# The stores of the input projection and of the gates issued from ScalarE's queue instead of the sync engine's

## The chip, the cores and the metric

One core of a Trainium2 chip runs the whole kernel. The metric is device time in microseconds (us) of one execution, from its first to its last work; below it is called the time. The core has engines that each take their own instructions in order: TensorE (PE, with PEld for its weight loads), VectorE (DVE), ScalarE (ACT), GpSimd (POOL) and the sync engine (SP), which computes nothing and only issues transfers. A transfer (DMA) is an instruction in one engine's queue; the data is moved afterwards by 16 DMA engines. An instruction that waits holds up everything behind it on its own engine.

## The reference

One layer of a decoder trunk, for 2048 tokens of width 1024, all in float32. Cut to what matters:

```python
mod = cond @ w_ada[l] + b_ada[l]
shift1, scale1, gate1, shift2, scale2, gate2 = jnp.split(mod, 6, axis=-1)
h = modulated_rmsnorm(x, norm_mix[l], shift1, scale1)
z = h @ w_in[l]
(gq, gk, gv, glow, gout, hq, hf, hi, hout,
 mqk, mv, mi, mf, mout) = jnp.split(z, IN_OFFSETS, axis=-1)
mixed = jnp.concatenate([gla_group(...), hgrn2_group(...), mlstm_group(...)], axis=-1)
x = x + gate1[:, None] * (mixed @ w_out[l])
h = modulated_rmsnorm(x, norm_mlp[l], shift2, scale2)
ff = jnp.square(jax.nn.relu(h @ w_ff1[l])) @ w_ff2[l]
x = x + gate2[:, None] * ff
return _rms(x) * final_norm
```

The three groups are recurrent token mixers (gated linear attention twice, mLSTM once), computed chunk by chunk. `z` is the input projection; its columns are activated (sigmoid, silu, a short convolution) before the mixers use them.

## The kernel before

The 2048 tokens are worked on in four quarters of 512. First comes the input projection of all four quarters (`inproj`), then the output projection and the feed-forward network of each quarter (`outproj`, `f1`, `f2`). The token mixing of a quarter (`block_pass`, `gates`, `chunk`) is emitted in small steps beside these dense products (`pump`), and a scheduler sets the final order on every engine from its own estimates of when each instruction could start; `ahead()` gives the dense products' casts and evacuations a preference over the mixing.

A dense product is done in three passes over operands split into a high and a low part. `weights` loads a piece into a buffer `raw` (two of them, L184, SP), ScalarE casts it to its high part in `wt` (three buffers, L176), and VectorE takes the rest (L177), which frees `raw`. The input projection has nine groups of columns for each quarter (f, q, conv, hout, gout, m, gqk, hi, gv). For one group, four PSUM banks `ps_ip` (four buffers of `psd`) collect the four tiles of 128 tokens over four pieces of weights; the next group's first products need the first bank back. `evac` empties a bank: ScalarE's activations and, for some groups, VectorE's products write a buffer `st` (three buffers for all groups), and a DMA `dma_s` stores it to DRAM (`zq`, `zv`, `zg`; `zm` from the convolution, and `gn` from `gla_gate`), where the token mixing later reads it. An `st` buffer is free for the next tile only when its store has landed. The stores are:

- group f: L765 and L766, behind VectorE's L763 and L764
- group q: L771, behind VectorE's L736 (`silu`) and L769; `gla_gate`: L869, behind ScalarE's L868
- conv: L751, behind VectorE's L750
- gout: L791, behind VectorE's L736; hout: L791, behind ScalarE's L787
- m: L779 and L780, gqk: L775, hi and gv: L784, all behind ScalarE's own copies and activations

Over the four quarters these are 184 transfers. The token mixing's loads and stores go through GpSimd's queue (`dma_m`), the loads of weights, of x and of the modulation weights through the sync engine's (`dma`). The norm of the next quarter is made beside the projection: L701 loads x (`m<-xq`) and ScalarE squares it in L208 and L210.

Of the kernel before, what the change touches and what calls it, by code (L numbers as in the profile page):

```python
# [101 lines left out]
def trunk(ctx, tc, I, out):  # L102
# [3 lines left out]
    dma_m = G.dma_start  # L106
    dma_s = nc.sync.dma_start

# [41 lines left out]
    def ahead():  # L150
        """What the dense products wait for goes before the token mixing in each engine's order."""
        return tc.high_priority(offset=lead[0])
# [4 lines left out]
    def late():  # L157
        """Products of the token mixing give way to so many instructions that came after them."""
        return tc.high_priority(offset=-LATE)

# [8 lines left out]
    def ln_exp(after):  # L169
        """The set with Exp and Ln, behind the activation after; what the caller adds to the stack runs behind it."""  # L170
        with tc.issue_after(after.ins):
            p_ = A.preload_act_table_set("natural_log_exp_and_others")
        return tc.issue_after(p_.ins)
# [5 lines left out]
    def weights(src, n, lp=None):  # L179
        """A [128, n] piece of weights as its two parts, [128, 2, n]."""  # L180
        with ahead():
            raw = wp.tile([P, 1024], F32, tag="raw", name="raw", bufs=2)
            r = raw[:, 0:n]
            dma(out=r, in_=src)  # L184
            wt = (lp or wp).tile([P, 2, 1024], F32R, tag="wt", name="wt", bufs=4 if lp else 3)
            split(wt[:, 0, 0:n], wt[:, 1, 0:n], r)
        return wt[:, :, 0:n]
# [10 lines left out]
    def modulate(hi, lo, src, rs, a_, b_, tmp=None):  # L198
        """hi + lo = src * a_ * rs + b_; the product goes to src's place if there is no tmp."""
        tmp = src if tmp is None else tmp  # L200
        V.scalar_tensor_tensor(out=tmp, in0=src, scalar=a_, in1=rs, op0=ALU.mult, op1=ALU.mult)
        A.activation(out=hi, in_=tmp, func=AF.Identity, bias=b_)  # L202
        V.scalar_tensor_tensor(out=lo, in0=tmp, scalar=b_, in1=hi.bitcast(F32), op0=ALU.add, op1=ALU.subtract)

    def sq_acc(sm, src, first, over=False):
        """Adds src ** 2 (to be kept in src's place if over) and its share of EPS to sm."""
        if first:
            return A.activation(out=sm, in_=src, func=AF.Square)  # L208
        sq = src if over else m5()[:, 0:src.shape[-1]]
        last = A.activation(out=sq, in_=src, func=AF.Square)  # L210
        V.scalar_tensor_tensor(out=sm, in0=sm, scalar=EPS / 7 * KT, in1=sq, op0=ALU.add, op1=ALU.add)
        return last

    def newton(x, y, t, scale):
        """One step of y towards (x * scale + EPS) ** -0.5; x and t are overwritten."""
        V.tensor_scalar(out=x, in0=x, scalar1=scale, scalar2=EPS, op0=ALU.mult, op1=ALU.add)
# [14 lines left out]

    # ---------------------------------------------------------------- conditioning
    ada_tags, acc_tags = [], ["prod", "sdt", "alb"]

    def ada(m, o, n, slow=False):
        """Channels o .. o + n of modulation vector m; slow: in steps and beside the rest, in the buffers of those."""
        h, o_ = divmod(o, 512)
# [37 lines left out]

    # ---------------------------------------------------------------- token mixing
    R.sd = [dp.tile([TQ, 576], F32, name=f"sd{q}") for q in range(NQ)]
# [15 lines left out]
    def block_pass(q, s):  # L293
        """Scores of tokens at most 15 apart within blocks of 16 tokens, for 48 channels per group."""
        c0 = (lambda g: 96 * g + 48 * s) if s < 2 else (lambda g: 384 + 48 * g)
# [26 lines left out]
    def gates(q):  # L322
        """mLSTM gate rows of a quarter (row 32 n + h: chunk n, head h): running stabiliser and what follows."""
        g = gm[q]
# [76 lines left out]
    def chunk(q, n, L, N):  # L401
        """Up to the normalised outputs of chunk n; N is the next chunk of the quarter."""
        nxt = (lambda f: f(q, n + 1, N)) if N else (lambda f: None)
        pt = lambda nm: psm.tile([P, 512], F32, tag="psm", name=nm)
        # channel-major q, k, f
        X = m1.tile([P, 15, 128], F32, tag="X", name="X")
# [64 lines left out]
        yield  # L471
        # mLSTM scores
        gT = [R.gT[:, i, n, :] for i in range(4)]
# [22 lines left out]
        yield  # L496
        # diagonal blocks of the gated groups' scores
        dsum = m1.tile([P, 12, 16], F32, tag="dsum", name="dsum")
# [7 lines left out]
        nxt(load_sd)  # L506
        # mLSTM output
        psi = pt("ps_mi")
# [35 lines left out]
        yield  # L544
        # scores of the gated groups
        heads = [(h // 2, 64 * (h % 2), 64) for h in range(6)] + \
# [69 lines left out]
        V.tensor_reduce(out=ss[:, 0:6], in_=sq, op=ALU.add, axis=AX.X)  # L616
        # norms, output gates
        with ln_exp(last):
# [35 lines left out]
    def both(a, b):  # L654
        """The steps of two independent generators by turns."""
        its = [a, b]
# [19 lines left out]

    # ---------------------------------------------------------------- input projection
    PASSES = ((0, 0), (0, 1), (1, 0))
# [33 lines left out]
    def h_stats_slow(q, res):  # L712
        """The same for quarter q in steps, its loads a step ahead."""
        sm = stat("sm", 2)
# [15 lines left out]
    def inproj(q, hts, nxt):  # L730
# [62 lines left out]
        def part(g, c0, n, ps, kk):  # L793
            """Two k-tiles' share of n columns of a group (of n // 128 channel tiles of the convolution)."""
            kind = GROUPS[g][0]
# [74 lines left out]

    # ---------------------------------------------------------------- output projection and feed-forward
    R.x1 = [dp.tile([P, KT, TQ], F32, name=f"x1{q}") for q in range(NQ)]

    def spare(spec, src):
        """Eight [128, 512] tiles in buffers that the chunks leave free, loaded from src."""
        ts = []
# [56 lines left out]
    def ffn_in(h2, q, xs, sm, last, lp=None):  # L933
        """The feed-forward's input into the list h2, in steps."""
        rs = stat("rs", 1)
# [35 lines left out]
    def f2_tile(hds, b, acc, w, dt, c):  # L971
        """Block b's share of channel tile dt for the tokens c of a quarter; w: from the number of a part to the part."""
        n, nf = c.stop - c.start, NF[b]
# [32 lines left out]
    def final_steps(q, acc):  # L1006
        """The final norm of a quarter, in steps."""
        sm = stat("sm", 2)
# [10 lines left out]
    def f2_last(lp, hds, acc):  # L1019
        """The last block and the final norm by halves of the tokens, the first norm beside the second half's products."""  # L1020
        ws = [w2_part(LB, i, lp) for i in range(NF[LB])]
# [14 lines left out]

    # ---------------------------------------------------------------- schedule
    prog = _K()
# [25 lines left out]
    def step():  # L1064
        """One step of the block passes (which run ahead) or of the chunks."""
        can_b = prog.blocks < prog.ready and prog.us >= prog.loaded
# [9 lines left out]
    def pump(us):  # L1076
        """Token mixing beside us of dense products, at the pace that the nearest deadlines ask for."""
        prog.us += us
# [110 lines left out]

# How the emission of the token mixing is paced beside the dense products, in us of the tensor engine's dense work  # L1190
# where the comment gives no other unit.
SLACK = (20, 60, 60, 60)    # by which a quarter's mixing is to be done before it is due
LAST = 1480                 # when the last quarter's mixing is due
FILL = 20.0                 # mixing emitted behind the first quarter's output projection
LOAD = 5.0                  # from a block pass's loads to its arithmetic
RUN = 0.2                   # share of the next quarter's block passes that goes beside a quarter's chunks
AHEAD = 60                  # instructions by which weights and evacuations go before the mixing
LATE = 20                   # instructions by which the mixing's products give way
STATS = 14                  # step of the input projection at which the next quarter's norm starts
BG = (24, 12, 20)           # steps of the input projection beside which the other modulation vectors are made  # L1200
EARLY = 3                   # feed-forward block of the last but one quarter behind which the last one's x1 is made
_OUT_SHAPE = (4, P, KT, TQ)
# [18 lines left out]
```

## Time and profile before

| what | value |
|---|---|
| time, median of 3 runs | 2723.67 us (2722.57 to 2724.44) |
| profiled execution: span | 2721.9 us |
| TensorE busy in the span | 2636.9 us (97%) |
| VectorE busy | 1792.1 us (66%) |
| ScalarE busy | 1231.6 us (45%) |
| GpSimd busy | 259.2 us (10%) |
| DMA | 401.76 MB, mean 148 GB/s |

The profiled execution is one run of its own; its own time is its span, 2721.9 us, which is 1.8 us below the median of the three timed runs. Times in the profile's rows count from the start of this span. A row of waits reads "who <- whom: us in total, times, longest"; a row of the timeline gives start, duration, engine, line, operation, tiles written and read, and in square brackets how long the engine sat idle before it and what released it. SPq is the sync engine's queue of transfers. The input projection fills the first 850 us or so; the rest is output projection and feed-forward.

### The profile page before, as it was taken

The page shows a single profiled execution, that of the slowest core. Times are in us where ns is not written, and L with a number is a line of the kernel's source. Part 1 is how long each engine was busy: PE and PEld are TensorE (multiplying, and loading weights), DVE is VectorE, ACT ScalarE, POOL GpSimd, SP SyncE. Part 2 cuts the span into 40 slices and gives each one's busy share as a digit, 9 for nine tenths or more (in the row PEclk, how much of TensorE's full clock was granted, in tenths as well). Part 3 has the DMA queues.
Part 4 walks back from the last instruction along what each step waited for, and adds up shares of the span by engine and source line. Part 5 has one row for each costly group of instructions (what it writes and reads, how often), then busy time and mean ns, then how long its engine had stood idle before and what let it go on. Part 6 is the DMA issues. An engine that isn't in the chain of part 4 may idle for free.

```text
span 2721.9 us, 39555 instructions
## 1 busy us (share of the span) xinstructions
PE 2636.9 (97%) x15050; PEld 2212.7 (81%) x15050; DVE 1792.1 (66%) x3345; ACT 1231.6 (45%) x2190; POOL 259.2 (10%) x434
## 2 busy tenths in 40 slices
PE   6999999999999999999999999999999999999998
PEld 5888898898888777788877888788877788888887
DVE  8785687977776877776887655457556556533335
ACT  4654445445543543454453445345445543433333
POOL 0101110020201102112110000100000000000000
PEclk9999999999999999999999999999999999999999
DMA  8776675585547424445454333344433245342332
GB/s 259 222 227 185 176 238 167 174 231 176 160 140 217 116 82 135 126 133 165 132 177 125 118 120 113 117 140 146 145 119 111 89 129 176 107 146 93 95 99 78
DMA packets 160200, 401.76 MB, mean 148 GB/s; under 512 B 20473, under 2 KB 60490, under 8 KB 160010
## 3 DMA queue, kind: packets, MB, share of 16 engines
q1 hardware_dynamic: 129338, 306.51, 35.7%
q0 software_dynamic: 30672, 92.73, 12.4%
q8 instruction: 118, 1.93, 0.3%
q14 instruction: 72, 0.59, 0.1%
HBM read 336.21 MB, written 62.95 MB: 147 GB/s over the span
## 4 chain that ended last, share of the span: by engine, by line
PE 50%; DVE 2%; ACT 1%; DMA 1%; issue 0%; DVEq 0%; ACTq 0%; SPq 0%
PE ps_f L155 40%; PE ps_op L155 5%; PE ps_a L163 2%; DVE wt L177 1%; DMA raw<-w 1%; PE ps_oh L163 1%; PE ps_og L163 1%; PE ps_t L167 0%; PE ps_x L167 0%; DVE acc L1000 0%; PE ps_mv L163 0%; ACT wt L176 0%; PE ps_uh L163 0%; PE ps_ug L163 0%; PE ps_ms L155 0%
## 5 line engine op out<-in xcount | busy, mean ns | idle before, releaser
L155 PE MATMUL ps_f<-ht,wt 128*128 128x512 f32 (+1 forms) x5472 | 1307.9, 393 | 4.8 <-ACT ht L202 4.8
L155 PEld LDWEIGHTS ps_f<-ht,wt 128*128 128x128 f32 x5472 | 1003.9, 189 | 213.4 <-ACT ht L202 5.0
L177 DVE TENSOR_TENSOR wt<-raw,wt 128x1024 fp32r<-128x1024 f32 (+3 forms) x436 | 498.8, 1145 | 412.8 <-ACT wt L176 411.7
L176 ACT CAST wt<-raw 128x1024 fp32r<-128x1024 f32 (+3 forms) x436 | 431.4, 990 | 640.1 <-PE ps_f L155 345.3
L155 PE MATMUL ps_ip<-wt,ht 128*128 128x384 f32 (+2 forms) x3072 | 604.5, 353 | 32.9 <-ACT st L782 8.7
L155 PEld LDWEIGHTS ps_ip<-wt,ht 128*128 128x128 f32 x3072 | 550.4, 191 | 61.1 <-ACT st L782 10.3
L982 DVE SCALAR_TENSOR_TENSOR acc<-ps_f,mod,acc 128x512 f32<-128x512 f32 (+1 forms) x200 | 145.2, 727 | 129.2 <-PE ps_f L155 128.4
L962 ACT ACTIVATE m<-ps_f 128x512 f32<-128x512 f32 x128 | 76.7, 599 | 318.5 <-PE ps_f L155 318.2
L155 PE MATMUL ps_f<-h,wt 128*128 128x512 f32 x768 | 181.4, 397 | 0.0
L155 PEld LDWEIGHTS ps_f<-h,wt 128*128 128x128 f32 x768 | 144.6, 188 | 35.6 <-issue 0.5
L155 PE MATMUL ps_op<-ht,wt 128*128 128x512 f32 x576 | 133.1, 393 | 5.7 <-ACT ht L176 3.8
L155 PEld LDWEIGHTS ps_op<-ht,wt 128*128 128x128 f32 x576 | 108.8, 190 | 29.2 <-ACT ht L176 3.9
L301 POOL DMA_DIRECT2D blk<-zq x144 | 93.6, 663 | 344.1 <-DVE prod L311 204.2
L567 DVE TENSOR_TENSOR td<-ps_a,td 128x384 f32<-128x384 f32 (+2 forms) x96 | 40.6, 423 | 110.8 <-PE ps_a L163 110.3
L311 DVE TENSOR_TENSOR prod<-blk 128x768 f32<-128x768 f32 (+3 forms) x192 | 111.2, 579 | 2.9
L312 DVE TENSOR_REDUCE Sd<-prod 128x48 f32<-128x768 f32 (+3 forms) x192 | 110.5, 575 | 3.0
L965 DVE TENSOR_TENSOR ht<-m,ht 128x512 fp32r<-128x512 f32 x128 | 88.1, 688 | 22.8 <-ACT m L964 22.3
L310 DVE TENSOR_TENSOR blk<-blk 128x720 f32<-128x720 f32 (+4 forms) x180 | 98.9, 549 | 0.0
L155 PE MATMUL ps_ip<-ht,wt 128*128 128x512 f32 x384 | 98.4, 404 | 0.0
L155 PEld LDWEIGHTS ps_ip<-ht,wt 128*128 128x128 f32 x384 | 71.4, 191 | 14.9 <-issue 0.7
L964 ACT ACTIVATE m<-m 128x512 f32<-128x512 f32 x128 | 81.0, 633 | 2.6
L963 ACT ACTIVATE ht<-m 128x512 fp32r<-128x512 f32 x128 | 81.1, 634 | 0.1
(393 smaller groups left out, 2627.2 us busy)
## 6 DMA issues: line engine op xcount, KB each, us to landing
raw<-w SPq DMA_DIRECT2D x256, 512.0 KB, 3.5
raw<-wg SPq DMA_DIRECT2D x100, 384.0 KB, 3.8
m<-wada SPq DMA_DIRECT2D x64, 256.0 KB, 3.7
raw<-wo SPq DMA_DIRECT2D x32, 512.0 KB, 3.5
m<-xq SPq DMA_DIRECT2D x56, 256.0 KB, 3.3
raw<-wg SPq DMA_DIRECT2D x28, 512.0 KB, 4.4
blk<-zq POOLq DMA_DIRECT2D x144, 96.0 KB, 6.1
zt<-zq POOLq DMA_DIRECT2D x48, 288.0 KB, 3.9
```

Source lines behind the costliest of these rows:

```text
L155: T.matmul(out=ps, lhsT=l, rhs=r, start=start, stop=stop)
L163: T.matmul(out=ps, lhsT=l, rhs=r, start=start, stop=stop)
L176: A.copy(out=hi, in_=src)
L177: V.tensor_tensor(out=lo, in0=src, in1=hi.bitcast(F32), op=ALU.subtract)
L301: dma_m(out=t[i][32 * g:32 * g + 32], in_=src)
L310: V.tensor_tensor(out=t[1][:, 0:n, :], in0=t[1][:, 0:n, :], in1=t[2][:, d:16, :], op=ALU.mult)
L311: V.tensor_tensor(out=prod[:, 0:n, :], in0=t[1][:, 0:n, :], in1=t[0][:, d:16, :], op=ALU.mult)
L312: V.tensor_reduce(out=s49[:, 0:n, d:d + 33:16], in_=prod[:, 0:n, :].rearrange("p j (u c) -> p j u c", c=16), op=ALU.add, axis=AX.X)
L963: A.activation(out=hd[:, 0], in_=r, func=AF.Square)
L964: A.activation(out=r, in_=r, func=AF.Square)
L965: V.tensor_tensor(out=hd[:, 1], in0=r, in1=hd[:, 0].bitcast(F32), op=ALU.subtract)
L982: V.scalar_tensor_tensor(out=acc[:, dt, c], in0=ps, scalar=mod[:, 40 + dt:41 + dt], in1=acc[:, dt, c], op0=ALU.mult, op1=ALU.add)
```

## The change

One name is bound to another queue: `dma_s`, which issues the stores listed above, becomes ScalarE's `dma_start`.

```diff
     V, A, G, T = nc.vector, nc.scalar, nc.gpsimd, nc.tensor
     dma = nc.sync.dma_start
     dma_m = G.dma_start
-    dma_s = nc.sync.dma_start
+    dma_s = A.dma_start
```

No arithmetic, no buffer and no size changes. Other lines of the diff only drop comments. Since the scheduler orders every engine anew, the order on the other engines shifts too.

ScalarE, quarter 0 (the whole piece is the group gqk and the start of the next quarter's norm): L773 and L774 empty a bank, L775 stores it, L208 squares the first piece of the next quarter's x, L176 casts weights.

```order
 L773 ACTIVATE st<-ps_ip 128x192
+L775 DMA zq_88<-st 128x2x192
 L774 COPY st<-ps_ip 128x192
-L208 ACTIVATE sm<-m_2597 128x512
-L176 CAST wt<-raw 128x768
+L176 CAST wt<-raw 128x768
+L775 DMA zq_88<-st 128x2x192
 L773 ACTIVATE st<-ps_ip 128x192
 L774 COPY st<-ps_ip 128x192
+L775 DMA zq_88<-st 128x2x192
+L208 ACTIVATE sm<-m_2597 128x512
+L176 CAST wt<-raw 128x768
```

The stores now stand among the evacuations, and L208 has moved from ahead of the fourth tile's evacuation to behind its store.

ScalarE, quarter 1, group gout (zg_97): L735 is the sigmoid that empties a bank, L226 and L227 belong to the next quarter's norm and need another table of functions.

```order
-L735 ACTIVATE st<-ps_ip 128x384 x3
-L176 CAST wt<-raw 128x1024
+L735 ACTIVATE st<-ps_ip 128x384 x2
+L791 DMA zg_97<-st 128x384 x2
+L735 ACTIVATE st<-ps_ip 128x384
+L176 CAST wt<-raw 128x1024
+L791 DMA zg_97<-st 128x384
+L735 ACTIVATE st<-ps_ip 128x384
 L226 ACT_TABLE_LOAD
 L226 ACTIVATE rs<-ps_ms 128x512
-L735 ACT_TABLE_LOAD
-L735 ACTIVATE st<-ps_ip 128x384
```

The fourth sigmoid has moved ahead of L226, and the table load that it needed behind L226 is gone.

The sync engine at the same place, groups hout and gout of quarter 1:

```order
-L791 DMA zg_97<-st 128x384 x2
-L184 DMA raw<-wg 128x768
-L791 DMA zg_97<-st 128x384 x2
-L184 DMA raw<-wg 128x1024 x4
-L791 DMA zg_97<-st 128x384 x3
-L184 DMA raw<-wg 128x768
-L791 DMA zg_97<-st 128x384
```

What remains there are the loads alone, in the same sequence.

## The prediction

> **What bounds the kernel now.** I read the busy times first, then the two halves of the span, then who waits for whom, and last the timeline around the gaps. The rows of the page and of the stretches (us, then for each engine busy time and instructions, last the granted clock, the DMA share and GB/s):
>
> ```profile
> PE 2636.9 (97%) x15050; PEld 2212.7 (81%) x15050; DVE 1792.1 (66%) x3345; ACT 1231.6 (45%) x2190; POOL 259.2 (10%) x434
> 0.00:850.00 850.00, 790.41 (x4755) 717.23 (x4756) 638.60 (x1283) 420.00 (x760) 108.34 (x182) 0.98 0.67 198
> 850.00:2721.90 1871.90, 1846.53 (x10297) 1495.47 (x10295) 1153.55 (x2063) 811.64 (x1430) 150.88 (x252) 0.99 0.40 125
> ```
>
> TensorE sets the time. Its work is not changed, so only its idle time (85 us) and its clock can move. In the projection, where all the stores are, it is idle for 850 - 790.4 = 59.6 us; ScalarE is busy 49% there. What ended that idle time, in the first 850 us:
>
> ```profile
> PE ps_ms L155 <- DVE sm L211: 13.8, 1, 13.8
> PE ps_ip L155 <- ACT st L782: 8.7, 5, 3.4
> PE ps_ip L155 <- ACT st L761: 7.7, 5, 2.8
> PE ps_ada L155 <- DVE ada_acc L256: 6.1, 2, 4.2
> PE ps_ip L155 <- ACT ht L202: 6.0, 4, 1.7
> PE ps_ip L155 <- DVE st L736: 5.8, 2, 4.8
> PE ps_ip L155 <- ACT st L774: 3.1, 1, 3.1
> ```
>
> The rows of L211, L256 and L202 (25.9 us) are the start, with no store in it. The rows with `st` are banks that came back late because a tile had not been emptied: 8.7 + 7.7 + 5.8 + 3.1 = 25.3 us. That is all that a change of the stores can win directly. Why were they late? ScalarE's own waits in the same stretch:
>
> ```profile
> ACT wt L176 <- PE ps_ip L155: 126.6, 51, 8.5
> ACT wt L176 <- DMA raw<-wg: 61.4, 23, 7.6
> ACT st L782 <- DMA zv<-st: 10.6, 5, 4.0
> ACT st L761 <- DMA zq<-st: 9.2, 6, 3.5
> ACT st L760 <- DMA zq<-st: 6.8, 4, 3.4
> ACT L735 <- DMA zg<-st: 4.2, 2, 3.4
> ```
>
> The last four rows are ScalarE standing before an evacuation because none of the three `st` buffers had landed: 30.8 us. The first row says that the casts of weights mostly run ahead of TensorE, so a small delay of a cast is covered. The largest gap shows the chain (ScalarE, then the sync engine, then TensorE; quarter 1, group gout):
>
> ```profile
> 322.99 1.28 ACT L226 ACT_TABLE_LOAD   x1
> 328.33 1.28 ACT L735 ACT_TABLE_LOAD   x1 [3.45 <-DMA zg<-st]
> 329.63 0.49 ACT L735 ACTIVATE st<-ps_ip 128x384 f32<-128x384 f32 x1
> 319.01 1.79 SPq L791 DMA_DIRECT2D zg<-st  x3
> 330.76 0.80 PE L155 MATMUL ps_ip<-wt,ht 128*128 128x512 f32 x1 [4.80 <-DVE st L736]
> ```
>
> The first three tiles' stores are issued from 319.01 on, the first lands only at about 328.3, the fourth sigmoid waits for it, pays a table load on top, and TensorE stands 4.80 us.
>
> **The change part by part.** It removes 184 transfers from the sync engine's queue and puts the same 184 into ScalarE's, each behind the activation or VectorE product that fills its buffer. Four terms follow.
>
> *Landing.* Now, the stores follow the weights' loads through one queue. What a store takes from issue to landing (rows of L766 and L791, then what the queues moved between 320 and 321 us: packets, MB, share of the DMA engines):
>
> ```profile
> DMA to landing us min/median/max: 1.9/2.8/5.3
> DMA to landing us min/median/max: 1.8/3.9/9.3
> q0 software_dynamic: 52, 0.10, 86.3%
> q1 hardware_dynamic: 3, 0.01, 4.2%
> ```
>
> Best case 1.8 us, worst 9.3. In the worst microsecond GpSimd's queue (q0) had the DMA engines and the sync engine's (q1), with load and stores in it, hardly moved. A queue of ScalarE's own may let a store pass the load ahead of it; whether it does, and how far it helps against q0, no row shows. Three gaps hang on a landing: the 4.80, and these two (quarter 3, groups f and gv):
>
> ```profile
> 648.12 0.49 ACT L761 ACTIVATE st<-ps_ip 128x384 f32<-128x384 f32 x1 [2.54 <-DMA zq<-st]
> 827.82 0.48 ACT L782 COPY st<-ps_ip 128x384 f32<-128x384 f32 x1 [4.00 <-DMA zv<-st]
> 648.66 11.61 PE L155 MATMUL ps_ip<-wt,ht 128*128 128x408 f32 x47 [2.71 <-ACT st L761]
> 828.36 13.82 PE L155 MATMUL ps_ip<-wt,ht 128*128 128x384 f32 x78 [1.17 <-ACT st L782]
> ```
>
> Together 4.80 + 2.71 + 1.17 = 8.7 us. Of the first, 1.28 us is the table load that the new order spares. Of the remaining 7.4 us I take half, 3.7, between nothing (landing as now) and all (landing near 1.8). Term: -5.0, bounds 0 and -8.7.
>
> A rule of the Trainium skill speaks against this term: by the page DMA: Bandwidth & Descriptors, section "Issuing engines are not separate DMA queues", transfers from any engine end up on the same 16 DMA engines and interleave, and spreading them saves issue time alone. By it the landing keeps its 3.9 us and the sum ends 3.7 us later; the trace's 4.2% against 86.3% agrees that the engines are shared, and does not show what a third queue gets.
>
> *Order.* Two gaps of quarter 0 come from x-loads that ScalarE waited for ahead of an evacuation:
>
> ```profile
> 182.98 0.63 ACT L208 ACTIVATE sm<-m 128x512 f32<-128x512 f32 x1 [4.75 <-DMA m<-xq]
> 184.82 13.79 PE L155 MATMUL ps_ip<-wt,ht 128*128 128x384 f32 x78 [3.05 <-ACT st L774]
> 199.55 0.63 ACT L210 ACTIVATE m<-m 128x512 f32<-128x512 f32 x1 [0.82 <-DMA m<-xq]
> 200.20 1.28 ACT L172 ACT_TABLE_LOAD   x1
> 202.02 3.47 PE L155 MATMUL ps_ip<-wt,ht 128*128 128x384 f32 x18 [3.41 <-ACT st L782]
> ```
>
> In the new order L208 stands behind the fourth tile's evacuation, so the 4.75 us wait no longer holds it: -3.05. At the second place the first L782 moves ahead of the last L210 (0.63) and of the table load (1.28): -1.9 of the 3.41. Term: -5.0, bounds 0 (another evacuation gets behind a load instead) and -6.5.
>
> *Clock.* After the two largest gaps the clock was low:
>
> ```profile
> 320.00:340.00 20.00, 15.20 (x53) 11.66 (x53) 7.90 (x11) 9.28 (x11) 0.07 (x1) 0.83 0.48 123
> 640.00:652.00 12.00, 9.29 (x48) 8.53 (x47) 9.42 (x21) 7.04 (x15) 0.55 (x1) 0.82 0.75 243
> ```
>
> Lost there: 20 x 0.17 + 12 x 0.18 = 5.6 us. If half of those gaps goes, half of this goes: -2.8, bounds 0 and -5.6.
>
> *ScalarE's load.* What an issue takes on the queue that issues it (min/median/max ns of L784 and L775):
>
> ```profile
> L784 SPq DMA_DIRECT2D zv<-st x32: 319/327/1263, 202.0 to 847.6; - x32
> L775 SPq DMA_DIRECT2D zq<-st x16: 359/403/553, 179.9 to 808.6; - x16
> ```
>
> At 0.33 us for most and 0.40 for the wider ones, 184 issues are about 184 x 0.34 = 63 us on ScalarE, which raises it from 420 to 483 of 850 us (57%). To that come its waits: 80 stores (f 32, q, conv and gout 16 each) follow a VectorE product. The one behind a sigmoid takes 0.55 us:
>
> ```profile
> L736 DVE TENSOR_TENSOR st<-ps_ip,st x32: 534/554/558, 91.3 to 756.7; 128x384 f32<-128x384 f32 x32
> ```
>
> If nothing stood between, that is 80 x 0.55 = 44 us more. What covers it: a piece of weights is six products per tile, 6 x 13.82 / 78 = 1.06 us, so a bank's evacuation may end 3 x 1.06 = 3.2 us behind its last product before TensorE stands; and in group f ScalarE now waits for landings anyway. What is queued behind a waiting store is the next tile's evacuation and the next cast, and TensorE waits for both. The cover is gone where ScalarE is already late, which by the waits is some ten places (the counts of the `st` rows are 5 + 5 + 2 + 1). With half a microsecond for each, one issue and part of a wait: 10 x 0.5 = +5; bounds 0 (all hidden) and 63 + 44 = +107 (nothing hidden). Those ends are far apart; I stay near the lower, because ScalarE is idle half of this stretch.
>
> The loads left alone in the sync engine's queue I cost at nothing: they wait for a free `raw`, so for VectorE, not for the queue, as its longest wait shows:
>
> ```profile
> SPq L184 <- DVE wt L177: 1615.7, 371, 22.4
> ```
>
> That cover would be gone where `raw` is free and a store holds the queue; its price lies inside the 61.4 us that ScalarE waits for `raw`. The stages behind 850 us keep their work; their new order I take as zero, within 3 us either way.
>
> Sum: -5.0 - 5.0 - 2.8 + 5 = -7.8 us on the 2721.9 us of the profiled execution, so 2714.1. That execution lay 1.8 us below the median of the runs, so the forecast is 2723.7 - 7.8 = **2716 us**.
>
> **The rivals.** *Nothing that counts.* The landing stays as long as it is, because GpSimd's queue holds the DMA engines and not the load ahead in the same queue: the term falls to the table load's 1.3 us, the clock's to nearly nothing, and -1.3 - 5.0 + 5 gives 2722. For it speaks the microsecond with 86.3%; against it that the stores stood behind a load of weights in their own queue. It is also what the page's rule would give.
>
> *ScalarE held by VectorE* (slower). The mechanism sits in groups f, q, conv and gout, 16 groups in all. It decides once ScalarE loses 0.8 us per tile to a store that waits for VectorE, since four tiles then use up the 3.2 us of slack. VectorE is 75% busy in this stretch and takes mixing in between; the two-product chain of f, at 0.55 us each with the sigmoid ahead, is above 0.8 us if nothing stands between. If half of the 16 groups then stands like the gap of quarter 3, 8 x 2.71 = 22 us, and half of the 2.2 us of clock lost around that gap, 8 x 1.1 = 9 us, less the 13.5 us (L761, L736) that stand there now: +17, with the order's -5 the time is 2736. Against it: the order puts sigmoids or casts of other tiles between product and store at most places.
>
> *A clean sweep.* All bounds on the good side, with the load at 0: -8.7 - 6.5 - 5.6 = -20.8 gives 2703.
>
> That the change does nothing can be left out: the order shows all stores moved.
>
> **How the numbers follow.** What a measurement of this kernel can tell from no change is 0.2%, 5.4 us. Forecast (2704 to 2718): 0.42. Clean sweep (below 2704): 0.05. Nothing that counts (2718 to 2729): 0.29. ScalarE held (above 2729): 0.24. So faster 0.47, same 0.29, slower 0.24. The likeliest case alone spans 2704 to 2718; the range that holds 8 in 10 goes from just below the clean sweep, 2702, to just beyond the slower rival, 2738.
>
> **What would show it.** Landing: stores under 3 us in the median for L791, and the waits of L735, L760, L761 and L782 for landings well under 30.8 us. Order: no gap behind L774 near 185 us. Load: ScalarE near 483 us busy plus issue time in its queue, and `st` rows of TensorE's waits below 25 us. Clock: 0.9 or more where it was 0.83. The forecast is wrong if TensorE's waits for `wt` or `st` grow beyond 30 us, or if landings stay at 3.9 us and ScalarE's waits with them.

## The result, and the profile after

The change is slower: 2749.22 us median (2745.9 to 2749.46) against 2723.12 us for the kernel before beside it. The ratio is 1.0086 with a 95% interval of 1.0071 to 1.0102, which is 26 us more, where 2716 us had been forecast, 8 less. A second measurement on another chip gave 1.0104 (1.0052 to 1.0155). The profiled execution is the timed run of 2749.21 us; its span is 2747.4 us, 1.8 us shorter than its time as in the kernel before, and 25.5 us longer than the span of before.

The page's busy times and its transfer queues (packets, MB, share of the 16 DMA engines' time):

```profile
PE 2646.1 (96%) x15050; PEld 2217.8 (81%) x15050; DVE 1795.3 (65%) x3345; ACT 1234.5 (45%) x2190; POOL 260.1 (9%) x434
q1 hardware_dynamic: 99770, 271.37, 31.7%
q10 hardware_dynamic: 29568, 35.14, 3.7%
```

TensorE does the same 15050 instructions. It is idle for 2747.4 - 2646.1 = 101.3 us (before 85.0, so +16.3) and busy for 9.2 us longer, which at equal work is a lower clock. q10 is new: ScalarE's queue, with the 35 MB of stores. The same stretches as before (us, then busy time and instructions of each engine, last granted clock, DMA share, GB/s), first of the change:

```profile
0.00:850.00 850.00, 775.07 (x4615) 698.77 (x4616) 631.28 (x1271) 411.43 (x742) 103.46 (x174) 0.97 0.64 190
200.00:300.00 100.00, 87.03 (x434) 79.84 (x433) 59.64 (x101) 38.89 (x64) 10.84 (x17) 0.90 0.65 187
```

and of the kernel before:

```profile
200.00:300.00 100.00, 94.10 (x496) 87.08 (x497) 70.48 (x124) 44.60 (x71) 10.83 (x17) 0.98 0.64 183
```

After 850 us TensorE has done 4615 instructions instead of 4755. At 775.07 / 4615 = 0.168 us each, it is 140 x 0.168 = 23.5 us behind: the loss lies in the input projection, and what comes behind it is as it was. In one stretch of 100 us the clock is at 0.90 instead of 0.98.

TensorE's waits in the projection (us in total, times, longest), and below them ScalarE's:

```profile
PE ps_ip L155 <- ACT st L782: 17.7, 6, 4.0
PE ps_ip L155 <- DVE wt L177: 9.4, 6, 3.7
PE ps_ip L155 <- ACT st L761: 5.7, 5, 1.5
PE ps_ms L155 <- DVE st L736: 2.9, 1, 2.9
```

```profile
ACT wt L176 <- DMA raw<-wg: 50.9, 22, 6.8
ACT st L782 <- DMA zv<-st: 14.2, 4, 6.0
ACT st L760 <- DMA zq<-st: 8.1, 4, 3.4
ACT st L761 <- DMA zq<-st: 6.7, 4, 2.8
ACT st L735 <- DMA zg<-st: 4.4, 2, 2.3
```

The row of L782 has doubled (8.7 before) and the splits of weights (L177) have become a wait (1.2 before); L736 has halved and the row of L774 has shrunk to less than a microsecond. ScalarE's four waits for a landing, 30.8 us before, are 33.4 us now; with the smaller rows of the same kind they are 54.0 us, and were 47.4. The landing has not become shorter. Issue and landing of the stores of L791 and L784 in the change (duration of an issue in ns, then issue to landing in us; first the two rows of L791):

```profile
L791 ACTq DMA_DIRECT2D zg<-st x32: 326/326/816, 127.3 to 786.3; - x32
DMA to landing us min/median/max: 2.2/3.9/7.8
L784 ACTq DMA_DIRECT2D zv<-st x32: 326/327/2159, 214.0 to 874.4; - x32
DMA to landing us min/median/max: 1.9/4.1/9.0
```

The medians of L791 are 3.9 us before and 3.9 us now, and an issue takes 0.33 us on either queue.

Two places carry most of what can be seen in quarter 0. The *second* is the plainer one, group hi (at 202 us before, where TensorE stood 3.41 us; 209 to 223 us now). ScalarE and its queue in the change:

```profile
209.57 0.47 ACT L782 COPY st<-ps_ip 128x384 f32<-128x384 f32 x1
214.02 0.63 ACT L210 ACTIVATE m<-m 128x512 f32<-128x512 f32 x1 [3.98 <-DMA m<-xq]
214.05 0.34 ACTq L784 DMA_DIRECT2D zv<-st  x1
214.56 0.46 ACT L782 COPY st<-ps_ip 128x384 f32<-128x384 f32 x1
215.05 0.34 ACTq L784 DMA_DIRECT2D zv<-st  x1
216.33 0.48 ACT L782 COPY st<-ps_ip 128x384 f32<-128x384 f32 x1
222.79 0.48 ACT L782 COPY st<-ps_ip 128x384 f32<-128x384 f32 x1 [5.98 <-DMA zv<-st]
```

and TensorE there:

```profile
210.09 1.49 PE L155 MATMUL ps_ip<-wt,ht 128*128 128x384 f32 x6 [3.91 <-ACT st L782]
215.07 4.21 PE L155 MATMUL ps_ip<-wt,ht 128*128 128x384 f32 x12 [3.49 <-ACT st L782]
223.32 2.93 PE L155 MATMUL ps_ip<-wt,ht 128*128 128x384 f32 x8 [4.04 <-ACT st L782]
```

A norm instruction (L210) now stands between the first and the second evacuation and waits 3.98 us for its load of x. The store of the first tile, whose copy ended at 210.04, and the second evacuation stand behind it. The fourth evacuation then waits 5.98 us for the first store to land. TensorE loses 3.91 + 3.49 + 4.04 = 11.4 us, and the low clock follows. The load itself comes late: it is the last of eight loads of x, issued at 207.0 us and landed 6.9 us later, where the kernel before issued it at 196.3 us and had it 3.2 us later. So it is issued 10.7 us later beside an evacuation that is 8 us later. In the sync engine's queue it now stands behind a load of weights (L184, 204.87) that it stood ahead of.

The *first* place is near 90 us. VectorE in the change, where the two splits that TensorE needs stand behind six products of the convolution:

```profile
84.89 0.75 DVE L256 SCALAR_TENSOR_TENSOR sm<-m,cond,sm 128x512 f32<-128x512 f32 x1 [2.10 <-DMA m<-wada]
85.56 4.06 DVE L747 SCALAR_TENSOR_TENSOR st<-cvr,pc,st 128x512 f32<-128x512 f32 x6
89.53 1.33 DVE L177 TENSOR_TENSOR wt<-raw,wt 128x816 fp32r<-128x816 f32 x2
```

TensorE stands 3.21 us there, and its 288th product of the projection (L155 into `ps_ip`) starts at 107.1 us instead of 99.6.

### The profile page after: what moved, and what is told of

It reads as the page before. It is cut to its first block, busy times and chain, and to the rows that moved or that the text cites. A ratio compares the mean times of both kernels' runs of the same rounds, so it can differ in the third digit from the quotient of the medians.

```text
span 2747.4 us, 39481 instructions
## 1 busy us (share of the span) xinstructions
PE 2646.1 (96%) x15050; PEld 2217.8 (81%) x15050; DVE 1795.3 (65%) x3345; ACT 1234.5 (45%) x2190; POOL 260.1 (9%) x434
## 4 chain that ended last, share of the span: by engine, by line
PE 51%; DVE 2%; ACT 1%; issue 0%; DVEq 0%
PE ps_f L155 42%; PE ps_op L155 3%; PE ps_a L163 2%; PE ps_oh L163 1%; PE ps_og L163 1%; PE ps_t L167 0%; DVE wt L177 0%; PE ps_x L167 0%; PE ps_ms L155 0%; DVE sm L211 0%; DVE prod L311 0%; PE ps_mv L163 0%; PE ps_qk L163 0%; PE ps_uh L163 0%; PE ps_ug L163 0%
## 5 line engine op out<-in xcount | busy, mean ns | idle before, releaser
L155 PE MATMUL ps_f<-ht,wt 128*128 128x512 f32 (+1 forms) x5472 | 1305.8, 393 | 4.6 <-ACT ht L202 4.6
L155 PEld LDWEIGHTS ps_f<-ht,wt 128*128 128x128 f32 x5472 | 1001.6, 188 | 213.2 <-ACT ht L202 5.1
L177 DVE TENSOR_TENSOR wt<-raw,wt 128x1024 fp32r<-128x1024 f32 (+3 forms) x436 | 498.4, 1145 | 419.0 <-ACT wt L176 408.4
L176 ACT CAST wt<-raw 128x1024 fp32r<-128x1024 f32 (+3 forms) x436 | 430.5, 990 | 645.1 <-PE ps_f L155 337.3
L155 PE MATMUL ps_ip<-wt,ht 128*128 128x384 f32 (+2 forms) x3072 | 611.8, 355 | 47.9 <-ACT st L782 17.7
L155 PEld LDWEIGHTS ps_ip<-wt,ht 128*128 128x128 f32 x3072 | 555.9, 193 | 78.4 <-ACT st L782 20.5
L155 PE MATMUL ps_f<-h,wt 128*128 128x512 f32 x768 | 181.4, 397 | 0.0
L155 PEld LDWEIGHTS ps_f<-h,wt 128*128 128x128 f32 x768 | 144.6, 188 | 35.6 <-issue 0.5
L155 PE MATMUL ps_op<-ht,wt 128*128 128x512 f32 x576 | 133.1, 393 | 3.8 <-ACT ht L176 3.8
L155 PEld LDWEIGHTS ps_op<-ht,wt 128*128 128x128 f32 x576 | 108.9, 190 | 27.0 <-ACT ht L176 3.9
L155 PE MATMUL ps_ip<-ht,wt 128*128 128x512 f32 x384 | 99.2, 407 | 0.0
L155 PEld LDWEIGHTS ps_ip<-ht,wt 128*128 128x128 f32 x384 | 72.2, 193 | 15.3 <-issue 0.7
```

The source lines that it names most:

```text
L155: T.matmul(out=ps, lhsT=l, rhs=r, start=start, stop=stop)
L176: A.copy(out=hi, in_=src)
L177: V.tensor_tensor(out=lo, in0=src, in1=hi.bitcast(F32), op=ALU.subtract)
```

## The experiments

Four theories were set against each other. **A**: ScalarE is held by stores that wait for VectorE (the rival of the prediction). **B**: any work and wait that an issue puts into ScalarE's in-order queue. **C**: the order that the scheduler now writes on all engines, whoever issues the stores. **D**: the queue in which the transfers run (their landing and what they share).

### Halves and quarters of the change

Two runs divide the stores by the engine that fills the buffer, two by the quarter of the tokens:

```diff
 e1_vector_fed: f, q, conv, gout on ScalarE
-                dma_s(out=zv[r, o:o + n], in_=s_)
+                dma(out=zv[r, o:o + n], in_=s_)
 (and so for m, gqk, hout, gn; e2_scalar_fed: the other way round)
 e3_quarter0 (e3b_quarters123: q > 0)
+        dma_s = A.dma_start if q == 0 else nc.sync.dma_start
```

> Only the 80 stores that follow a VectorE product (groups f, q, conv, gout) go to ScalarE's queue; the 104 that follow ScalarE's own copies stay with the sync engine. Theory A, ScalarE held by VectorE (the slower rival of the prediction): nearly the whole loss is here, 2743 to 2752 us. Theory B, in-order ScalarE: stores stand behind ScalarE's waits for loads and evacuations behind stores, whatever feeds them: about half of the loss, 2732 to 2740. Theory C, the scheduler's new order alone: no relation to what was moved, anything from 2715 to 2750.

> The complement: only the 104 stores behind ScalarE's own activations and copies (m, gqk, hi, gv, hout, the gate) go to ScalarE's queue. Theory A (held by VectorE): no loss, 2718 to 2727 us. Theory B (in-order ScalarE): about half of the loss, 2732 to 2740, with the dear gaps behind L782 near 210 us as in the change. Theory C (order alone): anything from 2715 to 2750.

> The stores of quarter 0 alone go to ScalarE's queue; quarters 1 to 3 store from the sync engine as before. In the change the projection is already 16 to 18 us late when quarter 0 ends, at its products' pace. If the loss is made where the stores are moved: 2738 to 2742 us, with the gaps behind L782 between 205 and 225 us again. If quarter 0's delay is caught up later or is an accident of the order: below 2732.

> The complement: the stores of quarters 1 to 3 alone go to ScalarE's queue. If the loss is made where the stores are moved: 2728 to 2734 us (some 8 us), quarter 0 as before. If the loss belongs to the queue as such, in proportion to the stores (138 of 184): 2740 to 2745.

Measured, as ratios to before: the 80 VectorE-fed stores 1.0047 (1.0027 to 1.0066), the 104 others 0.9991 (0.9973 to 1.001), quarter 0 alone 1.0029 (1.0007 to 1.0051), the other quarters 1.003 (1.0017 to 1.0043). That looks like theory A. But 11.5 + 0 us and 8.3 + 8.9 us both miss the whole's 26, and each of these kernels has an order of its own: of VectorE's 3345 instructions 842 stand elsewhere than before in the change, 502 in the first of these, 347 in the second, 278 and 716 in the quarters (counted by laying the two orders side by side). Which of order and queue was measured, these runs cannot say.

### ScalarE's time without the transfers, and weights first

In the first run ScalarE makes a small copy of the same buffer in place of each store, which the sync engine issues as before. The next two bring the cast and split of weights further ahead, in the change and, as a control, in the kernel before.

```diff
 e8_marker
-    dma_s = nc.sync.dma_start
+    def dma_s(out, in_):
+        A.copy(out=mark, in_=in_[:, 0:128] if len(in_.shape) == 2 else in_[:, 0, 0:128])
+        dma(out=out, in_=in_)
 e9_weights_after, e9_weights_before (in weights)
-        with ahead():
+        with tc.high_priority(offset=2 * lead[0]):
```

> The change once more, beside the others on one chip. All theories: 2740 to 2752 us. If it comes out below 2735, part of the loss seen first belongs to that chip, and the halves measured before are to be compared with this value.

> All 184 stores stay in the sync engine's queue; in the place of each, ScalarE makes a copy of 128 columns of the same buffer to a spare tile (about 0.3 us, with the same wait for the producer). Theory B (ScalarE's time and its in-order waits are the loss): 2738 to 2752 us, as the change. Theory D (where the transfer is queued, its landing and the semaphores shared with the loads, is the loss): 2718 to 2728. Theory C (order alone): anything from 2715 to 2750, with gaps at other places than the change's.

> The change, with the loads, casts and splits of weights put 120 instead of 60 instructions ahead in each engine's order, so that VectorE's split L177 no longer stands behind six products L747 of the convolution in quarter 0. Theory C (the new order is the loss, the queue is not): back to 2718 to 2730 us. Theories A and B (ScalarE's waits): 2738 to 2752, with the gaps behind `st` as before and only those behind `wt` (9.4 us) smaller.

> The kernel before with the same advance of the weights; a control for the run with the change. Theory C: a changed order alone moves the time by 5 us or more either way. Theories A and B: 2718 to 2728 us, no change.

The change again gave 1.0104, the marker 1.0019 (0.9992 to 1.0046), weights first 1.0089 (1.0051 to 1.0127) on the change and 1.0008 (0.9992 to 1.0024) on the kernel before. ScalarE with 184 more instructions that wait like the stores loses at most half of what the change loses. That speaks against B alone and does not settle it, since this kernel has an order of its own too. Weights first repairs nothing, so the late splits are not the whole of C.

### Order and queue, crossed

The two are separated by writing the order down. After the program is traced, each engine's instructions are tied, each to the one before it, in the order that the other kernel has; only the 184 stores are left out of it, and the scheduler places them in the queue of the engine that issues them. (In rows of kernels made like this the stores have line L107.)

```diff
+def keep_order(tc):
+    for e, z in ORDER.items():          # the order of the other kernel, engine by engine
...
+        for p_, i in zip(seq, seq[1:]):
+            tc.add_manual_dep(i, p_.name, edge(), reason="order")
 o_after_sp: the change's order, stores issued by the sync engine
 o_before_act: the order of before, stores issued by ScalarE
```

> The order of the change with the queue of before: each of TensorE, VectorE, ScalarE, GpSimd and the loads of the sync engine runs its instructions in exactly the order that they have in the change (an edge from each to the next), but the 184 stores are issued by the sync engine, placed there by the scheduler. Nothing is left out. Theory C (the new order alone costs the time): close to the change, 1.007 to 1.010 of before (2742 to 2750 us), with the stretch behind 205 us in group hi and the one near 90 us in group f slow as there. Theory B (the stores in ScalarE's in-order queue, their issues and waits): within 0.2% of before, since ScalarE issues nothing. Theory D (the transfers' own queue, not the order): the same, within 0.2% of before. A result of about 1.004 would mean that the two add.

> The order of before with the queue of the change: the five engines run everything but the stores in exactly the order of before, and the 184 stores are issued by ScalarE, placed among its instructions by the scheduler. Nothing is left out. Theory C (order alone): within 0.2% of before. Theories B and D (issues and waits on ScalarE, or the own queue): 1.006 to 1.010 of before (2740 to 2751 us). If both this kernel and its counterpart lie above 1.008, each order fits only its own queue; if both lie within 0.2%, only the two together cost the time.

The change's order with the old queue: 2749.73 us, ratio **1.01** (1.0082 to 1.0117). The old order with the change's queue: 2728.24 us, ratio **1.0011** (0.9998 to 1.0023). The order is the cost, and with three buffers the queue by itself is none that this measurement can tell. The second place in the first of these, with no store in ScalarE's queue; ScalarE, then TensorE:

```profile
210.53 0.47 ACT L782 COPY st<-ps_ip 128x384 f32<-128x384 f32 x1
216.07 0.63 ACT L210 ACTIVATE m<-m 128x512 f32<-128x512 f32 x1 [5.08 <-DMA m<-xq]
216.61 0.46 ACT L782 COPY st<-ps_ip 128x384 f32<-128x384 f32 x1
221.56 0.48 ACT L782 COPY st<-ps_ip 128x384 f32<-128x384 f32 x1 [2.70 <-DMA zv<-st]
```

```profile
211.05 2.29 PE L155 MATMUL ps_ip<-wt,ht 128*128 128x384 f32 x6 [4.87 <-ACT st L782]
217.12 4.21 PE L155 MATMUL ps_ip<-wt,ht 128*128 128x384 f32 x12 [3.78 <-ACT st L782]
222.09 8.12 PE L155 MATMUL ps_ip<-wt,ht 128*128 128x384 f32 x36 [0.76 <-ACT st L782]
```

The same L210 waits at the same place, and TensorE stands 4.87 + 3.78 + 0.76 = 9.4 us. In the other kernel, the old order with ScalarE's issues, the place is whole but for 0.89 us:

```profile
195.69 14.75 PE L155 MATMUL ps_ip<-wt,ht 128*128 128x384 f32 x84
211.33 13.81 PE L155 MATMUL ps_ip<-wt,ht 128*128 128x384 f32 x78 [0.89 <-ACT st L782]
```

### Which part of the order

Two runs take the change with the order of before up to behind the first place (the first 1020 of 19846 instructions, about 100 us) and up to behind the second (1700, about 225 us), and the change's order from there. A third takes the change and puts the L210 of the rows above and a table load behind the four evacuations on ScalarE; the order on the other engines stays that of the change.

```diff
 p_b1: ORDER = before[:1020] + what is left, as in the change
 p_b2: ORDER = before[:1700] + what is left, as in the change
 p_m2 (ScalarE, quarter 0, group hi)
 L782 st_1658
-L210 m5_2726
 L782 st_1667
-L172 table load
 L782 st_1676
 L782 st_1685
+L210 m5_2726
+L172 table load
```

> The change (stores issued by ScalarE) with the order of before for the first 1020 of the 19846 instructions of the schedule (some 100 us: quarter 0's groups f, conv and q), and from there the order of the change; stores placed by the scheduler. Nothing is left out. If the order's cost lies at its places, the first place's share (+8 to +10 us by the n-th projection product) goes: 1.006 of before, some 2740 us, and the gap that follows VectorE's splits near 90 us is gone while the three gaps behind L782 in group hi stay. If the cost is spread over the whole order, or the first place only delays what is made up later, it stays at 1.009 (2749 us).

> The same with the order of before for the first 1700 instructions (some 225 us: all of quarter 0's groups up to hi, both places), and from there the order of the change. Nothing is left out. If the cost lies at the two places of quarter 0 (+8 to +10 and +8 to +11 us): 1.002 to 1.003 of before, 2730 to 2733 us, the rest being the smaller places of the later quarters. If the cost is spread over the whole order: 1.008 or more (2746 us), since 92% of the instructions still stand in the change's order.

> The change with three instructions moved and nothing else: in quarter 0's group hi the last L210 of the next quarter's norm, VectorE's L211 behind it and the table load L172 stand behind the group's four evacuations (L782) instead of between them. Every other instruction keeps the change's order. Nothing is left out. If that one L210, which waits 3.98 us for its x-load in front of an evacuation and of a store, is what makes the second place slow: the gaps of 3.91, 3.49 and 4.04 us fall to about 3 us in all, the clock behind them stays up, and the time is 8 to 11 us below the change: 1.005 to 1.006 of before, 2738 to 2741 us. If the place is late because of the loads themselves (whoever waits for them), the wait only goes to another instruction and it stays at 1.009, 2749 us.

With the first place mended the ratio stays at 1.0099 (1.0077 to 1.0122); with both mended it is 1.0048 (1.0032 to 1.0064). The stretch with the second place carries about half of the loss. The first place's delay is in the trace of the change, but taking it away wins nothing in the end: the 288th product starts 6.5 us earlier than in the change, the 864th (behind the second place, which is nearly as bad there) 4.6 us earlier, and the 2016th 3.5 us later. Where that is lost again was not followed up, and this trace is of the slowest of the kernel's six runs (2744.5 to 2760.6 us).

The other half lies behind 225 us, and no run singles it out. The traces show its largest step, a *third* place near 580 us. VectorE and TensorE in the change:

```profile
576.67 0.75 DVE L256 SCALAR_TENSOR_TENSOR sm<-m,cond,sm 128x512 f32<-128x512 f32 x1 [2.38 <-DMA m<-wada]
582.10 0.95 DVE L177 TENSOR_TENSOR wt<-raw,wt 128x768 fp32r<-128x768 f32 x1
583.10 5.50 PE L155 MATMUL ps_ip<-wt,ht 128*128 128x384 f32 x21 [3.67 <-DVE wt L177]
```

VectorE waits for loads of the modulation weights ahead of a split that TensorE needs. In the kernel before TensorE does not stand there. From the 2304th to the 2400th product the lag behind the kernel before grows from 20.2 to 27.2 us in the change, from 18.1 to 27.8 us in its order with the old queue, and from 14.5 to 23.5 us with both places of quarter 0 mended. That this place makes up the other half is read from traces; no run takes it away.

Moving the L210 alone does not help: 2746.34 us, 1.0096 (1.0078 to 1.0113). The wait for x is gone from between the evacuations, and this stands in its place; ScalarE and its queue, then TensorE:

```profile
211.82 0.34 ACTq L107 DMA_DIRECT2D zv<-st  x1
212.20 0.48 ACT L782 COPY st<-ps_ip 128x384 f32<-128x384 f32 x1 [0.41 <-ACT st L782]
213.09 0.48 ACT L782 COPY st<-ps_ip 128x384 f32<-128x384 f32 x1 [0.41 <-ACT st L782]
222.30 0.48 ACT L782 COPY st<-ps_ip 128x384 f32<-128x384 f32 x1 [8.72 <-DMA zv<-st]
```

```profile
211.84 3.40 PE L155 MATMUL ps_ip<-wt,ht 128*128 128x384 f32 x18 [2.98 <-ACT st L782]
222.83 3.57 PE L155 MATMUL ps_ip<-wt,ht 128*128 128x384 f32 x10 [7.59 <-ACT st L782]
```

The first three stores leave at once, and the fourth evacuation waits 8.72 us until the first of them, issued at 211.82, has landed. TensorE stands 2.98 + 7.59 = 10.6 us instead of 11.4. The queues and some of the issues of that kernel between 205 and 225 us (packets, MB, share; then KB each and median us to landing):

```profile
q1 hardware_dynamic: 1152, 2.36, 45.0%
q0 software_dynamic: 720, 1.48, 33.4%
q10 hardware_dynamic: 576, 0.79, 13.2%
...
m<-wada SPq DMA_DIRECT2D x3, 256.0 KB, 5.3
zv<-st ACTq DMA_DIRECT2D x4, 192.0 KB, 10.5
```

45.0 + 33.4 + 13.2 = 91.6% of the DMA engines' time is taken, and a store takes 10.5 us to land. But a crowd is not what is new: in the kernel before, the same group fell into 97.3% (198 to 218 us), its first store landed after 3.2 us, and the fourth evacuation waited 1.79 us. Why the first store takes three times as long in this order stays open. Whichever instruction waits first here, the fourth of four tiles has to wait for the first of three buffers.

### One more buffer

```diff
-        st_ = lambda n, tag="st", bufs=3: ipool.tile([P, n], F32, tag=tag, name=tag, bufs=bufs)
+        st_ = lambda n, tag="st", bufs=4: ipool.tile([P, n], F32, tag=tag, name=tag, bufs=bufs)
 (and for ga; q_st4_after: order and queue of the change; q_st4_before: both of before;
 q_st4_before_act: the order of before, the queue of the change)
```

> The change's order and queue with four st buffers instead of three. Nothing is left out. ScalarE's waits for st to land (14.2 + 8.1 + 6.7 + 5.6 + 4.4 us and less) then all but vanish. If they carry the loss at the other places: the gap of 4.04 us at the second place and most of the rows of st go, 8 to 12 us less than the change, about 1.005 of before. If they stand off the path that sets the end: 1.009, as the change.

> The order and the queue of before with four st buffers instead of three. Nothing is left out. The prediction counted three gaps that hang on a landing, 4.80 + 2.71 + 1.17 us, with 4 us of clock behind them: if it sized them rightly, they go and the time is 8 to 12 us below before, 0.996 to 0.997, 2713 to 2716 us, which would beat both kernels. If the wait only goes to the next thing in line, within 0.2% of before.

> The order of before, the stores issued by ScalarE, and four st buffers: the kernel that beat both, with the change's queue. Nothing is left out. If the queue by itself counts for nothing (as the crossed run with three buffers says, 1.001): within 0.2% of the same kernel with the sync engine's queue, that is 0.995 to 0.999 of before, 2710 to 2720 us. If a queue of ScalarE's own lets stores land earlier once no evacuation waits for a buffer: below 0.995, under 2709 us. If ScalarE's issues and waits (184 x 0.33 us and the wait for VectorE) cost once the buffers no longer hide them: 1.000 or more.

In the change's order a fourth buffer takes the ratio from 1.0086 (and 1.0104) to **1.0024** (1.0012 to 1.0036): 17 to 22 us went through evacuations that waited for a landing (ScalarE's waits of that kind fall from 54.0 to 15.8 us). The second place with it; ScalarE, then TensorE:

```profile
211.65 0.63 ACT L210 ACTIVATE m<-m 128x512 f32<-128x512 f32 x1 [3.09 <-DMA m<-xq]
213.96 0.86 ACT L782 COPY st<-ps_ip 128x384 f32<-128x384 f32 x2
```

```profile
208.61 2.29 PE L155 MATMUL ps_ip<-wt,ht 128*128 128x384 f32 x6 [4.19 <-ACT st L782]
212.70 32.60 PE L155 MATMUL ps_ip<-wt,ht 128*128 128x384 f32 x171 [1.80 <-ACT st L782]
```

L210 still waits, but the third and fourth evacuations follow each other, and 4.19 + 1.80 = 6.0 us are left of the 11.4.

In the kernel before, the fourth buffer is worth 2715.18 us, ratio **0.9972** (0.9962 to 0.9983). It beats both kernels. So the order of before loses 7.3 us in the same way, and of what the change loses *against it* the buffers explain some 10 to 15 us; with four buffers in both, 1.0024 against 0.9972 remains, 14 us for order and queue together. In the trace of the change's order with four buffers the third place is still there (the lag grows from 7.0 to 16.2 us). With ScalarE's queue in that kernel the gain is gone: 2723.47 us, 1.0 (0.9986 to 1.0015), measured on another chip against its own runs of before. The two intervals just fail to meet, so the queue may cost 0.3% there; with three buffers it cost 0.1%, within its interval of nothing.

### Other orders

Two runs, stores with the sync engine, get a new order by a cause that has nothing to do with the stores:

```diff
 e4_order_b
-LATE = 20
+LATE = 24
 e4_order_a
-AHEAD = 60
+AHEAD = 64
```

> A reorder that has nothing to do with the stores: the stores stay in the sync engine's queue, and the products of the token mixing give way to 24 later instructions instead of 20, so the scheduler writes another order (about 900 of TensorE's, 400 of VectorE's and 170 of ScalarE's instructions stand elsewhere than before). Nothing is left out. If any fresh order of this kernel costs (the order of before being a lucky one): 1.004 or more, 2733 us and up. If the cost belongs to the few places that the change's order made worse: within 0.2% of before.

> A second reorder that has nothing to do with the stores: weights and evacuations go 64 instead of 60 instructions ahead of the mixing; the stores stay with the sync engine. Nothing is left out. If the order of before is a lucky one, this costs like the first such reorder: 1.003 to 1.007 of before, 2732 to 2743 us. If that one was an exception: within 0.2%, or faster.

The first is at 1.0059 (1.0038 to 1.0079; some 400 of VectorE's and 900 of TensorE's instructions moved), the second at 1.0002 (0.999 to 1.0015). The second hardly counts as an order of its own: 65 of VectorE's instructions moved, 8 of ScalarE's and none of TensorE's. In the control of weights first, 548 and 265 moved, and it stayed at 1.0008. So a fresh order does not always cost, but it can cost 16 us for no reason in the edit, and the number of VectorE's moved instructions does not tell.

## Why the prediction was wrong

The sum had four terms: -5.0 - 5.0 - 2.8 + 5.

**Landing (-5.0, bounds 0 and -8.7).** Half of it came, and hardly by landings. At the three gaps TensorE waits 2.90, 1.38 and 1.95 us in the change, 6.2 instead of 8.7, the first of them now behind VectorE's L736 and no landing; 1.28 of these 2.5 us can be the table load that the new order spares. The step that failed is "of the remaining 7.4 us I take half". The landing is 3.9 us in the median for L791 as before, ScalarE's four waits for it went from 30.8 to 33.4 us, and the largest of them grew from 4.0 to 6.0. The rule that was weighed against it (the Trainium skill, DMA: Bandwidth & Descriptors, "Issuing engines are not separate DMA queues") holds here, and the trace agrees with it: 3.9 us on either queue. In the old order with ScalarE's queue the waits for landings, small rows included, did fall, from 47.4 to 38.8 us, and the time did not. The gaps were also less the landing's than the term had it. With a fourth buffer in the kernel before, 3.35 us of the 4.80 stay (the fourth sigmoid then stands behind a cast that waits 4.09 us for its weights), 1.67 of the 2.71 stay, and the 1.17 go: 3.7 of the 8.7 hung on a buffer. The 7.3 us that this kernel gains come in good part from elsewhere.

**Order (-5.0, bounds 0 and -6.5).** This step carries the miss. Half of it came: behind L774 TensorE stands 0.56 us instead of 3.05. At the second place the first L782 did move ahead of the last L210, as the rows said. But L210 was priced at its 0.63 us of work; its wait for x, 0.82 us before, became 3.98, and now stood in front of the second evacuation and of the first store: TensorE stood 11.4 us instead of 3.4, where 1.9 were to be won. The loads left in the sync engine's queue were costed at nothing; that the last x was issued later there and took 6.9 us instead of 3.2 is what this wait is made of. The bound of 0 ("another evacuation gets behind a load instead") named the mechanism and gave it no price. More than that, the term looked at two places of an order in which 842 of VectorE's instructions had moved. The whole of it, measured with the stores in their old queue, is 1.01, that is +27 us (22 to 32).

**Clock (-2.8, bounds 0 and -5.6).** At the two places that were priced it came as forecast: 0.91 from 330 to 350 us and 0.89 from 666 to 678 us (the same places, moved by the lag), where it had been 0.83 and 0.82, so 20 x 0.09 + 12 x 0.11 = 3.1 us are lost there instead of 5.6. But around the second place, where the gaps grew, it went from 0.98 to 0.90 over 100 us, another 8 us that no term held.

**ScalarE's load (+5, bounds 0 and +107).** About right. The change's queue in the old order is 1.0011, +3 us (-0.5 to +6), with whatever the landing wins or loses in it. With four buffers the same queue costs 0.28%, so three buffers may hide a part.

**Behind 850 us (0, within 3).** Right: 23.5 of the 25.5 us are there by 850 us.

Put together, the two crossed runs give 27 + 3 = 30 us against the 26 measured, inside the intervals.

**The rivals.** The slower one, "ScalarE held by VectorE", had the sign and 2736 us, but not the mechanism: the old order has the same 80 stores behind VectorE's products in ScalarE's queue and costs 0.1%. What the VectorE-fed half cost in its own run, 1.0047, came with that run's order. "Nothing that counts" was right about the landing. That none of the rivals was the order itself is the gap in the list, and why the range ended at 2738: the only loss in it was priced through ScalarE's queue.

**What would show it.** The signs that were named turned the right way round: landings at 3.9 us and TensorE's rows for `wt` and `st` beyond 30 us (17.7 + 9.4 + 5.7 + 2.9 = 35.7) were given as what would prove the forecast wrong, and they did. The sign for the clock (0.9 or more where it was 0.83) came true, at a place that did not decide.

## What to carry to other kernels

Where a scheduler writes the order, an edit to one queue is an edit to every engine's order: before believing a gain or a loss, cross the two, the new queue in the old order and the old queue in the new one. An order is not priced by the waits of the old trace; an instruction that waits for a load costs what the load is late at its new place, and everything behind it on that engine pays. Where evacuations wait for stores to land, one more buffer is worth more than another queue: here 0.3% on the kernel before, and 17 to 22 us of the change's loss in its own order.

## What had not been expected

An order made by another setting, with no store moved, costs 16 us, and a single wait of 4 us taken out of the way at the worst place wins nothing, since the wait for the landing behind it was nearly as long. The stores' landing of 10.5 us, with 91.6% of the DMA engines' time taken, is nearly three times their median of 3.9 to 4.1, while at 97.3% in the kernel before the first store of the group lands in 3.2 us; the share alone does not tell. The load of x is late at that place although the sync engine has 184 issues fewer: it is issued later, behind a load of weights that it used to precede. What else held it back was not followed up.
